# A trunk step whose late stage is queued in another order, with convolution taps issued singly and block products reordered

## The chip, the cores and the metric

The kernel runs on one core of a Trainium2 chip. The metric is the device time of one execution in microseconds (us). The engines that matter are TensorE (PE in the profile; its weight loads are PEld), VectorE (DVE), ScalarE (ACT), GpSimd (POOL) and SyncE (SP), whose queue issues most transfers. Each engine works through its own queue strictly from first to last; semaphores hold an instruction back until what it reads is written and what it overwrites has been read.

## The reference

One inference step of a two-layer trunk for 576 tokens (512 of a prompt, 64 of eight sample sequences), 1024 wide. Layer 0 is a gated short convolution, layer 1 an mLSTM with four heads of 512; each branch is 2048 wide and gated by a SiLU path z.

```python
for layer in range(DEPTH):                       # DEPTH = 2
    hnorm = rmsnorm(x, norm_w[layer])
    out = short_conv_mixer(...) if layer % 2 == 0 else mlstm_mixer(...)
    x = x + out
y = rmsnorm(x, final_norm_w)

# layer 0                                        # layer 1
b, c, xa, z = split(h @ w_in, 4)                 xm, z = split(h @ w_in, 2)
y = b * conv(c * xa) * silu(z)                   xc = silu(conv(xm) + conv_b)
out = y @ w_out                                  q, k, v = xc @ w_q, xc @ w_k, xm @ w_v
                                                 # per head: scores with decays, running state C, n, m
                                                 num = w_inter * (q @ C) + S @ v
                                                 C_new = decay * C + kw.T @ v
                                                 out = (layernorm(num / den) * onorm + skip * xc) * silu(z)
                                                 out = out @ w_out
```

The states C (4 heads x 8 samples of 512 x 512) are read, updated and written.

## The kernel before

Activations lie transposed: a tile is 128 channels by 576 tokens. Every fp32 product is made of three products of rounded parts (hi·hi, hi·lo, lo·hi), which give fp32 accuracy: a tile is cast to `hi` on ACT (L159, L202, L250) and the rest `lo` or `wl` is taken on DVE (L160, L203, L251). A chunk of weights (1024 x 128) times an activation is 48 matmuls on PE (`products`, L222), 8 blocks by three parts by two token ranges.

Stages by time in the trace: projection of layer 0 until about 375 us; its output projection until about 512; xm of layer 1 until about 611; V until about 835; K and Q until about 1290; and then the **late stage**: the z tiles of layer 1 (`z_tile`), scores, numerators (`num`), the outputs per head (`head_out`), the updates of the state C streamed through the core in 512 KB halves (load `c<-cs`, product `r` L1122, update on DVE L1123, store `cs_out`), the final states of the prompt (`cp`), and the output projection in two halves (`first_half` adds the residual x1s, `second_half`).

Names that matter below:

- `block_pair` (L290 to L365) makes two chunks of a product with seven block products instead of eight (38 pairs in layer 0, V, K and Q). Each product is 12 matmuls (L304) into one of four PSUM buffers `b0` to `b3`; DVE sums tiles of weights and adds the PSUM buffers up in 128 x 288 pieces (`tt`). `plain` (L368) makes a chunk of an ordinary product beside it.
- `work` is a queue of small closures; `run(n)` pops n of them, and `products` pops one behind the blocks named in `pops`, so that small work lands between matmuls.
- `conv_steps` / `conv`: the first tap of a convolution runs on ACT, the other three on DVE (L440 on the prompt, L442 on the samples). In layer 1, `mix` does one tile's convolution.
- `stack` (L1024 cast on ACT, L1025 on DVE) makes the parts of a tile stand beside each other; `value_stack(h)` makes `vst` for the state products, `key_stack` makes `kst`, from which `pn` (L1061) and the masked keys `km` (ACT, L1069) follow.
- `head_out(h, et)` transposes sample rows (`hb`, L1243) and prompt rows (`ha`, L1252) on PE, moves them to a tile y on ACT (L1246, L1254), adds skip * xc (DVE, L1257; `ld<-xcs` is its load) and multiplies by z (L1258). `split_out(f)` then splits that y (L159, L160), as an operand of the output projection.
- The large accumulators `acc` have two PSUM buffers; a z tile's is emptied by one ACT instruction (L875, SiLU once the SiLU table is loaded, before that a copy), the ones of the output projection by a DVE add (L1284).

The program is not issued as written. A scheduler lists the instructions of each engine in an order that it finds with a model of its own; what is written sets priorities and the allocation of buffers. The order of the changed program can therefore differ at places that the diff doesn't name, and stay where the diff moves code.

Of the kernel before, what the change touches and what calls it, by code (L numbers as in the profile page):

```python
# [21 lines left out]
NH = 4  # L22
# [45 lines left out]
def trunk(tc, io):  # L68
    nc = tc.nc
    ctx = ExitStack()  # L70
    with ctx:
# [103 lines left out]
        def run(n=1):  # L175
            for _ in range(min(n, len(work))):
                work.popleft()()

        stream = deque()
        clock = [0.0, None]  # L180

# [108 lines left out]
        def block_pair(c1, c2, fs, xs, out1, out2, add, mid=None, then=None, pops=0):  # L290

            a11, a12, a21, a22, s1, s2 = ahead_of.pop((c1, c2))
            o11, o12, o21, o22 = out1[:, 0:HT], out1[:, HT:NT], out2[:, 0:HT], out2[:, HT:NT]
            pu = X(name="pu")
            p, u = pu[:, 0:HT], pu[:, HT:NT]
            tt = nc.vector.tensor_tensor

            def product(bank_, w, form, start):  # L300
                for j in range(4):
                    hi, lo = fs[j][form]
                    for i, (a, x) in enumerate(((w[0], hi), (w[0], lo), (w[1], hi))):
                        nc.tensor.matmul(bank_, a[:, j, :], x, start=(start and j == 0 and i == 0), stop=(j == 3 and i == 2),  # L304
                                         skip_group_check=True)

            b1 = block("p6")
            product(b1, parts_of(s2), "t2", True)
            b0 = block("p1")
            product(b0, parts_of(a11), "b11", True)  # L310
            nc.scalar.copy(p, b0)
            run(pops)
            b2 = block("p5")
            product(b2, parts_of(s1), "t1", True)
            if add:
                tt(o12, o12, b1, ALU.subtract)
                tt(o12, o12, p, ALU.add)
            else:
                tt(o12, p, b1, ALU.subtract)
            run(pops)  # L320
            product(b0, parts_of(a12), "b21", False)
            if add:
                tt(o22, o22, b2, ALU.subtract)
                tt(o22, o22, p, ALU.subtract)
            else:
                tt(o22, p, b2, ALU.add)
            tt(a21, a21, a11, ALU.add)
            tt(s2, s2, a12, ALU.add)
            run(pops)
            product(b1, parts_of(a21), "t3", False)  # L330
            run(pops)
            b3 = block("p4")
            product(b3, parts_of(a22), "t4", True)
            tt(u, b1, p, ALU.subtract)
            if add:
                tt(o22, o22, b1, ALU.add)
            else:
                tt(o22, b1, o22, ALU.subtract)
            run(pops)
            product(b2, parts_of(s2), "b22", False)  # L340
            if mid:
                mid()
            if then:
                block_weights(*then)
            if add:
                tt(o11, o11, b0, ALU.add)
                tt(o21, o21, b3, ALU.add)
                tt(o21, o21, u, ALU.add)
            elif xs is None:
                nc.scalar.copy(o11, b0)  # L350
                tt(o21, b3, u, ALU.add)
            else:
                plain(b3, b1, c2 + 1, xs, False)
                tt(o21, b3, u, ALU.add)
                tt(o22, b1, o22, ALU.add)
                plain(b0, b2, c1 + 1, xs, None)
                nc.scalar.copy(o11, b0)
            tt(o12, o12, b2, ALU.add)

        def plain(ba, bb, chunk, xs, start):  # L360

            w = weights(chunk)
            for k in range(8):
                (hi, lo), (xh, xl) = w[k // 4], xs[k]
                for i, (a, x) in enumerate(((hi, xh), (hi, xl), (lo, xh))):  # L365
                    for b, t in ((ba, 0), (bb, HT)):
                        new = start if t == 0 or start is None else True
                        nc.tensor.matmul(b, a[:, k % 4, :], x[:, t:t + HT], start=bool(new) and k == 0 and i == 0,  # L368
                                         stop=(k == 7 and i == 2), skip_group_check=True)
                if k % 2:  # L370
                    run()

        def gemm_pair(c1, c2, fs, xs, out1, out2, plain_first=False, mid=None, then=None):

# [242 lines left out]
        for f in range(NW):  # L617
# [14 lines left out]
            elif f % 2:  # L632
                fm.append(forms(us[f - 1], u))

            def mix(f=f, u=u, ext=ext, ext_f=ext_f):
                cv = T(name="xc")
                conv(cv, u, ext_f, [col(f"cb{j}", f) for j in range(4)])
                nc.gpsimd.tensor_copy(cpb[:, f, :], u[:, NP - 3:NP])
                nc.scalar.activation(cv, cv, AF.Silu, bias=col("cbias", f))
                store_act(out=xcs[f], in_=cv)  # L640
                if f % 4 == 3:
                    store(out=io["exb_out"][f // 4], in_=ext)
                if f == NW - 1:
                    store(out=io["cpb_out"], in_=cpb)

            work.append(mix)
            if f >= LAG:
                run()
            if f == NW - 3:
                block_weights(96, 98)  # L650

# [54 lines left out]
        for h in range(NH):  # L706
            vt = []
            for dt in (0, 2):
# [10 lines left out]
                if 4 <= f < 12:  # L719
                    work.extend(lambda f=8 + f - 4 + i: xc.append(split(later_tile(f))) for i in range(2))  # L720
            work.append(lambda h=h, vt=vt: gates(h, vt))

        Sc, qcs = {}, {}
        far = [dram.tile([P, 512], F32, name=f"far{i}") for i in range(3)]
# [143 lines left out]
                nc.scalar.copy(z, flat(acc))  # L868
            zs[f // 4].append(z)

        table, last_silu = [], []

        def silu(out, src):
            with tc.issue_after(table[0]):
# [2 lines left out]
        def silu_table():  # L877

            with tc.issue_after(last_exp[0].ins):
                table.append(nc.scalar.preload_act_table_set("silu_and_others").ins)  # L880
            for h in range(NH):
                for t in zs[h]:
                    silu(t, t)


        keep = T(name="keep")
# [268 lines left out]
        def preps(h):  # L1155
            work.extend(lambda jt=jt: prep_values(h, jt) for jt in range(4))
            work.extend(lambda t=t: prep_scores(h, t) for t in range(4))

        def weighted_keys(h, dt):

# [75 lines left out]
        def head_out(h, et):  # L1236

            nums = heads[h]["nums"]
            f = 4 * h + et
            if et == 0:  # L1240
                pb = bank("hb")
                for i in range(4):
# [33 lines left out]

        x2 = []

        def first_half(m):
            x = T(name="x")  # L1280
            load(out=x, in_=x1s[m])
            acc = mm("acc")
            products(acc, weights(208 + 2 * m), y2[0:8], True, True)
            nc.vector.tensor_tensor(x, flat(acc), x, ALU.add)  # L1284
            x2.append(x)

# [33 lines left out]
        for h in range(NH):  # L1320
# [49 lines left out]
            for dt in range(2):  # L1370
                fetch_keys(h + 1, dt)
            work.extend(lambda h=h, et=et: head_out(h, et) for et in range(4))
            if h == 2:
                work.extend(lambda f=f: split_out(f) for f in range(8, 12))
            z_tile((0, 1, 2, 3, 4, 5, 6, 7))
            if h == 2:
                work.append(lambda: "vst" in heads[3] or value_stack(3))
                run(len(work))
                for m in range(FH):
                    first_half(m)  # L1380


        run(len(work))
        for m in range(FH + FI, 4):
            first_half(m)
        for et in range(4):
            head_out(3, et)
        for f in range(12, 16):
            split_out(f)
        for m in range(4, KD):  # L1390
            first_half(m)

        with tc.issue_after(last_silu[0]):
            nc.scalar.preload_act_table_set("abs_reciprocal_sqrt_and_small")
# [199 lines left out]
```

## Time and profile before

| | us |
|---|---|
| median of three runs (1714.5, 1715.65, 1722.03) | 1715.65 |
| the profiled execution | 1715.56 |
| its span, first to last instruction | 1713.5 |
| PE busy | 1669.4 |
| DVE busy | 1105.3 |
| ACT busy | 685.3 |
| mean granted clock of PE, share of full speed | 0.987 |

PE is busy for 97% of the span, so the time is that of its matmuls, plus the 44 us in which it stands, plus the time in which it runs at a lower granted clock. The window tables used below give, for each stretch, its length, the busy us of each engine with the number of its instructions (x), the granted clock (1.00 is full speed), the busy share of the 16 DMA engines and GB/s.

### The profile page before, as it was taken

How to read it: one execution, taken by the hardware profiler on the slowest of the kernel's cores; microseconds unless marked ns; L12 is line 12 of the kernel's file. 1: busy time of each engine (PE TensorE's matmuls, PEld its weight loads, DVE VectorE, ACT ScalarE, POOL GpSimd, SP SyncE). 2: the span in 40 equal slices, each digit the busy share in tenths (PEclk: the TensorE clock that was granted, in tenths of full speed). 3: DMA queues.
4: the chain of work that ended last, by engine and by line, in shares of the span. 5: the costliest groups of instructions: out<-in, count | busy, mean ns of one | idle time of the engine just before them, and what ended most of it. 6: DMA issues, size and time to landing. Idle time of an engine off the chain costs nothing.

```text
span 1713.5 us, 30944 instructions
## 1 busy us (share of the span) xinstructions
PE 1669.4 (97%) x12315; PEld 1591.1 (93%) x12315; DVE 1105.3 (65%) x2078; ACT 685.3 (40%) x1252; POOL 107.7 (6%) x241
## 2 busy tenths in 40 slices
PE   9999999999999999999999999999999998898998
PEld 8999999999999999999999889899899787898898
DVE  6977877774436896555846345355468556778755
ACT  5433343342323553433534233233246455554421
POOL 0000000000000001000110010000021000000000
PEclk9999999999999999999999999999999899999999
DMA  5223322223432434434423552642745588797973
GB/s 193 74 83 99 103 86 85 90 73 137 141 115 87 141 122 151 138 111 154 152 88 120 188 178 87 219 154 62 271 161 195 201 280 286 247 361 249 362 276 105
DMA packets 107487, 275.23 MB, mean 161 GB/s; under 512 B 11056, under 2 KB 33456, under 8 KB 107344
## 3 DMA queue, kind: packets, MB, share of 16 engines
q1 hardware_dynamic: 91984, 255.95, 45.0%
q10 hardware_dynamic: 15360, 17.32, 2.9%
q8 instruction: 97, 1.59, 0.4%
q14 instruction: 46, 0.38, 0.1%
HBM read 211.13 MB, written 62.09 MB: 159 GB/s over the span
## 4 chain that ended last, share of the span: by engine, by line
PE 88%; DMA 5%; DVE 4%; ACT 2%; issue 1%; SPq 0%; POOL 0%; DVEq 0%; ACTq 0%; POOLq 0%
PE acc L222 34%; PE p L304 24%; PE p L368 16%; DMA c<-cs 2%; PE qa L759 2%; PE r L1122 2%; DMA cs_out<-c 1%; DMA wr<-wts 1%; PE g L661 1%; PE num L1175 1%; PE ta L680 1%; PE cp L1175 1%; PE num L1176 1%; PE s L778 1%; PE blk L368 1%
## 5 line engine op out<-in xcount | busy, mean ns | idle before, releaser
L222 PE MATMUL acc<-hi,wh 128*128 128x256 f32 (+1 forms) x1520 | 331.7, 299 | 11.1 <-ACT z L875 6.8
L222 PE MATMUL acc<-hi,wl 128*128 128x256 f32 (+1 forms) x1520 | 330.8, 299 | 0.0
L222 PE MATMUL acc<-lo,wh 128*128 128x256 f32 (+1 forms) x1520 | 330.2, 299 | 0.0
L202 ACT CAST wh<-wr 128x512 fp32r<-128x512 f32 x286 | 176.5, 621 | 328.6 <-PE acc L222 174.5
L304 PE MATMUL p<-hi,wh 128*128 128x288 f32 x968 | 286.7, 299 | 3.7 <-ACT wh L250 2.1
L304 PE MATMUL p<-lo,wh 128*128 128x288 f32 x968 | 284.5, 295 | 0.0
L304 PE MATMUL p<-hi,wl 128*128 128x288 f32 x968 | 279.2, 295 | 1.2 <-DVE wl L251 1.2
L222 PEld LDWEIGHTS acc<-hi,wh 128*128 128x128 f32 x1520 | 257.8, 191 | 16.0 <-ACT z L875 7.0
L203 DVE TENSOR_TENSOR wl<-wr,wh 128x512 fp32r<-128x512 f32 x286 | 195.8, 689 | 118.4 <-ACT wh L202 115.8
L222 PEld LDWEIGHTS acc<-hi,wl 128*128 128x128 f32 x1520 | 257.8, 191 | 2.2 <-issue 1.2
L222 PEld LDWEIGHTS acc<-lo,wh 128*128 128x128 f32 x1520 | 257.7, 191 | 0.7 <-issue 0.5
L250 ACT CAST wh<-wr 128x512 fp32r<-128x512 f32 x152 | 94.5, 622 | 258.4 <-PE p L368 116.7
L304 PEld LDWEIGHTS p<-hi,wh 128*128 128x128 f32 x968 | 181.9, 188 | 7.8 <-ACT wh L250 3.7
L304 PEld LDWEIGHTS p<-lo,wh 128*128 128x128 f32 x968 | 182.4, 188 | 0.0
L304 PEld LDWEIGHTS p<-hi,wl 128*128 128x128 f32 x968 | 179.9, 188 | 1.4 <-DVE wl L251 1.4
L368 PE MATMUL p<-hi,wh 128*128 128x288 f32 x736 | 169.9, 299 | 0.0
L368 PE MATMUL p<-lo,wh 128*128 128x288 f32 x736 | 166.9, 294 | 0.0
L368 PE MATMUL p<-hi,wl 128*128 128x288 f32 x736 | 166.4, 296 | 0.2 <-DVE wl L203 0.2
L251 DVE TENSOR_TENSOR wl<-ws,wh 128x512 fp32r<-128x512 f32 x114 | 78.7, 691 | 119.6 <-ACT wh L250 119.4
L250 ACT CAST wh<-ws 128x512 fp32r<-128x512 f32 x114 | 70.8, 621 | 187.8 <-PE p L368 108.3
L251 DVE TENSOR_TENSOR wl<-wr,wh 128x512 fp32r<-128x512 f32 x152 | 104.9, 691 | 52.3 <-ACT wh L250 50.5
L368 PEld LDWEIGHTS p<-hi,wh 128*128 128x128 f32 x736 | 120.8, 188 | 14.7 <-issue 11.2
(371 smaller groups left out, 2557.2 us busy)
## 6 DMA issues: line engine op xcount, KB each, us to landing
wr<-wts SPq DMA_DIRECT2D x222, 512.0 KB, 3.6
c<-cs SPq DMA_DIRECT2D x112, 512.0 KB, 5.8
cs_out<-c SPq DMA_DIRECT2D x64, 512.0 KB, 6.7
x<-xT SPq DMA_DIRECT2D x16, 288.0 KB, 4.1
xcs<-xc ACTq DMA_DIRECT2D x16, 288.0 KB, 2.2
x<-xcs SPq DMA_DIRECT2D x16, 288.0 KB, 4.1
x<-x1s SPq DMA_DIRECT2D x16, 288.0 KB, 4.5
ld<-xcs SPq DMA_DIRECT2D x16, 288.0 KB, 7.5
```

The lines of the kernel that those rows point to most:

```text
L202: last_act[0] = nc.scalar.copy(hi, raw[:, 4 * i:4 * i + 4, :]).ins
L203: nc.vector.tensor_tensor(lo, raw[:, 4 * i:4 * i + 4, :], hi.bitcast(F32), ALU.subtract)
L222: nc.tensor.matmul(acc[:, o:o + j - i], a[:, k % 4, :], x[:, i:j], start=(first and k == 0 and p == 0), stop=(last and k == 7 and p == 2))
L250: last_act[0] = nc.scalar.copy(hi, src).ins
L251: nc.vector.tensor_tensor(lo, src, hi.bitcast(F32), ALU.subtract)
L304: nc.tensor.matmul(bank_, a[:, j, :], x, start=(start and j == 0 and i == 0), stop=(j == 3 and i == 2), skip_group_check=True)
L368: nc.tensor.matmul(b, a[:, k % 4, :], x[:, t:t + HT], start=bool(new) and k == 0 and i == 0, stop=(k == 7 and i == 2), skip_group_check=True)
L661: nc.tensor.matmul(g[32 * j:32 * j + 32, 0:b - a], w[:, 32 * j:32 * j + 32], tiles[j][:, a:b], start=True, stop=True)
L680: nc.tensor.transpose(pa[:, 128 * it:128 * it + 128], t[:, 128 * it:128 * it + 128], ident)
L759: nc.tensor.matmul(st["q"][32 * g:32 * g + 32, :], st["qp"][dt // 2][:, dt % 2, 128 * u + 32 * g:128 * u + 32 * g + 32], ct[g // 2][:, g % ...
L1122: nc.tensor.matmul(r, kst[2 * i + j][:, 128 * dt:128 * dt + 128], vst[:, 0:512], start=True, stop=True)
L1175: nc.tensor.matmul(acc[:, 256:512], w, b[:, 0:256], **ends)
```

## The change

Six edits: (A) `block_pair` forms its products in the order t2, b11, t1, t3, b21, t4, b22 and shares one sum `u`, which leaves out one 128 x 288 operation on DVE for each pair. (B) The loads of x1s for `first_half` are issued one chunk ahead. (C) The SiLU of the seven z tiles that were made before the SiLU table is loaded is written in `head_out`. (D) `value_stack(h)` is queued in `preps(h)`. (E) Of heads 2 and 3, `head_out` and `split_out` are queued differently around the last z tiles and the `first_half` calls. (F) The convolution taps of layer 1 are queued singly in `slow` and taken by `drip()`, five per tile while xm is made, and one per two blocks in `plain`.

```diff
+        slow = deque()
+        def drip():
+            if slow:
+                slow.popleft()()
...
+            tt(a21, a21, a11, ALU.add)
+            product(b1, parts_of(a21), "t3", False)
             run(pops)
+            tt(u, b1, p, ALU.subtract)
             product(b0, parts_of(a12), "b21", False)
+            tt(s2, s2, a12, ALU.add)
             if add:
                 tt(o22, o22, b2, ALU.subtract)
-                tt(o22, o22, p, ALU.subtract)
+                tt(o22, o22, u, ALU.add)
             else:
-                tt(o22, p, b2, ALU.add)
-            tt(a21, a21, a11, ALU.add)
-            tt(s2, s2, a12, ALU.add)
-            run(pops)
-            product(b1, parts_of(a21), "t3", False)
+                tt(o22, u, b2, ALU.subtract)
             run(pops)
             b3 = block("p4")
             product(b3, parts_of(a22), "t4", True)
-            tt(u, b1, p, ALU.subtract)
-            if add:
-                tt(o22, o22, b1, ALU.add)
-            else:
-                tt(o22, b1, o22, ALU.subtract)
             run(pops)
             product(b2, parts_of(s2), "b22", False)
...
                 if k % 2:
                     run()
+                    drip()
...
-            def mix(f=f, u=u, ext=ext, ext_f=ext_f):
-                cv = T(name="xc")
-                conv(cv, u, ext_f, [col(f"cb{j}", f) for j in range(4)])
+            def begin(f=f, u=u, ext_f=ext_f, cv=cv):
+                cv.append(T(name="xc"))
+                cv.extend(conv_steps(cv[0], u, ext_f, [col(f"cb{j}", f) for j in range(4)]))
+                cv[1]()
...
-            work.append(mix)
+            slow.extend([begin] + [lambda s=s, cv=cv: cv[s]() for s in (2, 3, 4)] + [end])
             if f >= LAG:
-                run()
+                for _ in range(5):
+                    drip()
...
-            for h in range(NH):
-                for t in zs[h]:
-                    silu(t, t)
+            raw_z.extend(t for h in range(NH) for t in zs[h])
...
+            work.append(lambda: "vst" in heads[h] or value_stack(h))
...
+            if zs[h][et] in raw_z:
+                silu(zs[h][et], zs[h][et])
...
-        def first_half(m):
-            x = T(name="x")
-            load(out=x, in_=x1s[m])
+        def first_half(m, pops=()):
+            if m + 1 < KD:
+                fetch_x(m + 1)
+            x, = fetched.pop(("x1", m))
             acc = mm("acc")
-            products(acc, weights(208 + 2 * m), y2[0:8], True, True)
+            products(acc, weights(208 + 2 * m), y2[0:8], True, True, pops)
...
-            if h == 2:
-                work.extend(lambda f=f: split_out(f) for f in range(8, 12))
             z_tile((0, 1, 2, 3, 4, 5, 6, 7))
             if h == 2:
                 work.append(lambda: "vst" in heads[3] or value_stack(3))
-                run(len(work))
+                work.extend(lambda f=f: split_out(f) for f in range(8, 12))
+                fetch_x(0)
                 for m in range(FH):
-                    first_half(m)
+                    first_half(m, (0, 2, 4, 6))
...
-        for et in range(4):
-            head_out(3, et)
-        for f in range(12, 16):
-            split_out(f)
+        work.extend(lambda et=et: head_out(3, et) for et in range(4))
+        work.extend(lambda f=f: split_out(f) for f in range(12, 16))
         for m in range(4, KD):
-            first_half(m)
+            first_half(m, (0, 3, 6))
+        run(len(work))
```

How the instructions stand on an engine before and after is shown at three places. Numbers in names tell buffers apart and differ between the two programs; line numbers of the changed kernel are 2 to 14 higher.

ACT's queue around the last z tile, before (about 1543 to 1556 us in the trace). `z_17838<-acc` empties the last z tile's accumulator; `hi<-y` are the casts of `split_out(8)` to `split_out(11)`:

```order
L1246 ACTIVATE y_17737<-hb_17726,cols 128x64
L1254 ACTIVATE y_17731<-ha_17739,cols 128x512
L1254 ACTIVATE y_17733<-ha_17753,cols 128x512
L1254 ACTIVATE y_17735<-ha_17767,cols 128x512
L202 CAST wh_18128<-wr_18126 128x512
L159 CAST hi_17804<-y_17731 128x576
L1254 ACTIVATE y_17737<-ha_17781,cols 128x512
L159 CAST hi_17814<-y_17733 128x576
L202 CAST wh_18132<-wr_18126 128x512
L159 CAST hi_17824<-y_17735 128x576
L159 CAST hi_17834<-y_17737 128x576
L875 ACTIVATE z_17838<-acc_17709 128x576
```

The same place after (`z_17794<-acc` is the last z tile):

```order
L1256 ACTIVATE y_17715<-hb_17704,cols 128x64
L884 ACTIVATE z_17794<-acc_17677 128x576
L1406 ACT_TABLE_LOAD
L1264 ACTIVATE y_17709<-ha_17717,cols 128x512
L1031 CAST sth_17818<-ld_17386 128x512
L1264 ACTIVATE y_17711<-ha_17731,cols 128x512
L1264 ACTIVATE y_17713<-ha_17745,cols 128x512
```

The emptying of the last z tile has moved from behind all four casts of y to in front of the moves of the `ha` transposes; the four `hi<-y` casts stand 13 to 17 rows behind it.

PE's queue in the output projection of the first halves, before (1626 to 1633 us): the last matmul of one `first_half`, the row `pn`, ten state products `r` in a row (six of them shown), and the first matmul of the next `first_half`:

```order
L222 MATMUL acc_18675<-hi_17699,wl_18683 128x320
L1061 MATMUL pn_18789<-seln,kst_18784 128x4 x4
L1122 MATMUL r_18807<-vst_17840,km_18329 128x512
L1122 MATMUL r_18811<-vst_17840,km_18330 128x512
L1122 MATMUL r_18846<-vst_17840,km_18331 128x512
...
L1122 MATMUL r_18960<-vst_17845,km_18800 128x512
L1122 MATMUL r_18995<-vst_17845,km_18797 128x512
L1122 MATMUL r_18999<-vst_17845,km_18798 128x512
L222 MATMUL acc_18755<-hi_17205,wh_18758 128x256
```

The same place after, with the last matmuls before the row and the first behind it:

```order
L228 MATMUL acc_18711<-hi_17642,wl_18719 128x320
L1068 MATMUL pn_18749<-seln,kst_18744 128x4 x4
L1129 MATMUL r_18767<-vst_17595,km_18293 128x512
L1129 MATMUL r_18771<-vst_17595,km_18294 128x512
L228 MATMUL acc_18711<-hi_17667,wh_18718 128x256
...
L228 MATMUL acc_18711<-hi_17694,wl_18719 128x320
L1129 MATMUL r_18810<-vst_17595,km_18295 128x512
L228 MATMUL acc_18818<-hi_17167,wh_18821 128x256
```

The `r` now come in ones and twos with 5 to 30 matmuls of an accumulator between them.

DVE's queue in the first pair of V, before (621 to 627 us): convolution taps (L440, L442) of four tiles between sums of the block products (L334, L338) and the low part of a weight (L203):

```order
L440 SCALAR_TENSOR_TENSOR xc_7199<-xm_6661,cols,xc_7199 128x511
L442 SCALAR_TENSOR_TENSOR xc_7199<-ext_6368,cols,xc_7199 128x64
L334 TENSOR_TENSOR pu_7021<-p_7022,pu_7021 128x288
L338 TENSOR_TENSOR v_7020<-p_7022,v_7020 128x288
L440 SCALAR_TENSOR_TENSOR xc_7224<-xm_6740,cols,xc_7224 128x511
L442 SCALAR_TENSOR_TENSOR xc_7224<-ext_6679,cols,xc_7224 128x64
L440 SCALAR_TENSOR_TENSOR xc_7248<-xm_6817,cols,xc_7248 128x511
L442 SCALAR_TENSOR_TENSOR xc_7248<-ext_6679,cols,xc_7248 128x64
L440 SCALAR_TENSOR_TENSOR xc_7175<-xm_6584,cols,xc_7175 128x510
L442 SCALAR_TENSOR_TENSOR xc_7175<-ext_6368,cols,xc_7175 128x64
L203 TENSOR_TENSOR wl_7160<-wr_7153,wh_7159 128x512
```

The same pair after:

```order
L442 SCALAR_TENSOR_TENSOR xc_7160<-xm_6570,cols,xc_7160 128x510
L444 SCALAR_TENSOR_TENSOR xc_7160<-ext_6354,cols,xc_7160 128x64
L442 SCALAR_TENSOR_TENSOR xc_7244<-xm_6647,cols,xc_7244 128x510
L209 TENSOR_TENSOR wl_7214<-wr_7207,wh_7213 128x512
L444 SCALAR_TENSOR_TENSOR xc_7244<-ext_6354,cols,xc_7244 128x64
L442 SCALAR_TENSOR_TENSOR xc_7160<-xm_6570,cols,xc_7160 128x509
L444 SCALAR_TENSOR_TENSOR xc_7160<-ext_6354,cols,xc_7160 128x64
L257 TENSOR_TENSOR wl_7288<-ws_7135,wh_7287 128x512
```

Before, the first pair of V holds the taps of six tiles; after, it holds those of two, the second pair those of two, and the third and the fourth those of one each.

## Rows read from the trace of the kernel before

**Rows 1.** The page: the busy time of each engine (busy us, share of the span, instructions).

```profile
PE 1669.4 (97%) x12315; PEld 1591.1 (93%) x12315; DVE 1105.3 (65%) x2078; ACT 685.3 (40%) x1252; POOL 107.7 (6%) x241
```

**Rows 2.** The waits of PE over the whole span, longest total first: line that waited <- line waited for, us in total, times, longest.

```profile
PE acc L222 <- ACT z L875: 6.8, 1, 6.8
PE num L1200 <- DVE vst L1025: 3.1, 1, 3.1
PE r L1122 <- ACT y L1254: 2.7, 1, 2.7
PE pn L1061 <- DVE kst L1025: 2.4, 2, 1.8
PE r L1122 <- DVE c L1123: 2.3, 10, 0.6
...
PE acc L222 <- DVE x L1284: 1.5, 1, 1.5
...
PE p L304 <- DVE wl L251: 1.2, 1, 1.2
```

**Rows 3.** Windows around the last z tile (window, length, PE, PEld, DVE, ACT and POOL busy us with instructions, granted clock, DMA share, GB/s).

```profile
1545.00:1550.00 5.00, 4.33 (x32) 4.01 (x30) 5.00 (x8) 3.75 (x7) 0.00 (x0) 1.00 0.58 226
1550.00:1555.00 5.00, 0.00 (x0) 0.00 (x0) 4.76 (x8) 0.82 (x2) 0.00 (x0) 0.84 0.43 116
1555.00:1560.00 5.00, 3.87 (x16) 3.87 (x17) 2.88 (x5) 4.19 (x8) 0.00 (x0) 0.50 0.98 336
1560.00:1565.00 5.00, 5.00 (x37) 4.87 (x36) 2.59 (x6) 3.70 (x6) 0.53 (x1) 0.98 0.09 34
```

**Rows 4.** The timeline there (start, duration, engine, line, operation, and in brackets the idle time of that engine before it and what ended it).

```profile
1554.01 0.76 DVE L1258 TENSOR_TENSOR y<-y,z 128x576 f32<-128x576 f32 x1
...
1554.86 0.67 ACT L159 CAST hi<-y 128x576 fp32r<-128x576 f32 x1 [3.32 <-DVE y L1258]
...
1555.43 0.64 ACT L875 ACTIVATE z<-acc 128x576 f32<-128x576 f32 x1
...
1556.13 0.85 PE L222 MATMUL acc<-hi,wh 128*128 128x256 f32 x2 [6.79 <-ACT z L875]
```

**Rows 5.** Windows over the end of the first halves of the output projection and behind it; columns as in rows 3.

```profile
1615.00:1620.00 5.00, 3.50 (x18) 3.19 (x19) 5.00 (x8) 0.55 (x2) 0.00 (x0) 0.83 1.04 390
1620.00:1625.00 5.00, 5.00 (x33) 4.96 (x33) 4.03 (x7) 1.20 (x2) 0.00 (x0) 0.83 0.95 349
1625.00:1630.00 5.00, 3.10 (x13) 1.83 (x12) 3.56 (x7) 3.70 (x6) 0.00 (x0) 0.85 0.99 366
1630.00:1635.00 5.00, 5.00 (x13) 3.19 (x14) 4.89 (x8) 0.00 (x0) 0.00 (x0) 0.50 1.03 410
...
1650.00:1700.00 50.00, 50.00 (x375) 49.39 (x374) 28.44 (x60) 12.82 (x27) 0.00 (x0) 1.00 0.40 130
```

**Rows 6.** The chain of work that ended last, in the same place, in order of time: start, us, what.

```profile
1580.11 8.59 DMA cs_out<-c
1588.77 6.43 DMA c<-cs
1595.20 6.32 DMA cs_out<-c
...
1602.02 7.08 DMA ld<-xcs
1609.19 0.83 DVE y L1257
...
1616.17 0.76 DVE x L1284
...
1629.10 4.00 PE r L1122 x6
...
1659.55 0.47 PE r L1122 x2
1660.02 3.99 PE acc L222 x30
```

**Rows 7.** Windows in the first pair of V; columns as in rows 3.

```profile
630.00:635.00 5.00, 4.83 (x36) 4.59 (x35) 5.00 (x12) 2.11 (x4) 0.00 (x0) 1.00 0.13 22
635.00:640.00 5.00, 3.82 (x26) 3.20 (x25) 5.00 (x13) 3.07 (x5) 0.00 (x0) 1.00 0.78 274
640.00:645.00 5.00, 3.94 (x30) 3.71 (x29) 5.00 (x11) 4.08 (x7) 2.56 (x2) 1.00 0.44 127
...
650.00:850.00 200.00, 198.65 (x1536) 194.32 (x1535) 125.42 (x232) 77.71 (x140) 13.44 (x33) 1.00 0.44 136
```

**Rows 8.** The timeline at the SiLU table load and at a set of sample numerators (`sample_numerators`, L1200); columns as in rows 4.

```profile
1411.77 4.13 ACT L875 ACTIVATE z<-z 128x576 f32<-128x576 f32 x7
...
1417.95 1.08 PE L1122 MATMUL r<-vst,km 128*128 128x512 f32 x2 [2.72 <-ACT y L1254]
...
1465.51 0.61 ACT L1024 CAST sth<-ld 128x512 fp32r<-128x512 f32 x1
...
1468.17 0.58 PE L1200 MATMUL num<-vst,pst 128*128 128x256 f32 x1 [3.13 <-DVE vst L1025]
```

**Rows 9.** A stretch of layer 0 by its window (columns as in rows 3), and the operation of DVE that the pairs share: line, engine, operation, count: shortest/median/longest ns.

```profile
100.00:400.00 300.00, 300.00 (x2260) 300.00 (x2260) 225.64 (x406) 117.45 (x199) 7.24 (x13) 1.00 0.30 92
...
L334 DVE TENSOR_TENSOR pu<-p,pu x38: 449/456/469, 63.4 to 1269.3; 128x288 f32<-128x288 f32 x38
```

More of the change, by code (lines that the diff above doesn't have):

```diff
@@ L633, in trunk, with end @@
                 fm.append(forms(us[f - 1], u))
-            def mix(f=f, u=u, ext=ext, ext_f=ext_f):
-                cv = T(name="xc")
-                conv(cv, u, ext_f, [col(f"cb{j}", f) for j in range(4)])
+            cv = []
+            def begin(f=f, u=u, ext_f=ext_f, cv=cv):
+                cv.append(T(name="xc"))
+                cv.extend(conv_steps(cv[0], u, ext_f, [col(f"cb{j}", f) for j in range(4)]))
+                cv[1]()
+            def end(f=f, u=u, ext=ext, cv=cv):
                 nc.gpsimd.tensor_copy(cpb[:, f, :], u[:, NP - 3:NP])
-                nc.scalar.activation(cv, cv, AF.Silu, bias=col("cbias", f))
-                store_act(out=xcs[f], in_=cv)
+                nc.scalar.activation(cv[0], cv[0], AF.Silu, bias=col("cbias", f))
+                store_act(out=xcs[f], in_=cv[0])
                 if f % 4 == 3:
@@ L721, in trunk @@
             work.append(lambda h=h, vt=vt: gates(h, vt))
+        assert not slow
         Sc, qcs = {}, {}
@@ L869, in z_tile @@
             zs[f // 4].append(z)
-        table, last_silu = [], []
+        table, last_silu, raw_z = [], [], []
         def silu(out, src):
@@ L1277, in trunk, with fetch_x @@
         x2 = []
-        def first_half(m):
-            x = T(name="x")
-            load(out=x, in_=x1s[m])
+        def fetch_x(m):
+            fetch(("x1", m), x1s[m], n=NT)
+        def first_half(m, pops=()):
+            if m + 1 < KD:
+                fetch_x(m + 1)
+            x, = fetched.pop(("x1", m))
             acc = mm("acc")
-            products(acc, weights(208 + 2 * m), y2[0:8], True, True)
+            products(acc, weights(208 + 2 * m), y2[0:8], True, True, pops)
             nc.vector.tensor_tensor(x, flat(acc), x, ALU.add)
```

## The prediction

> **What bounds the kernel now.** I read the page first, for the engine that sets the time: PE is busy for 1669.4 of the 1713.5 us span, DVE for 65% of it [rows 1]. The change removes no matmul, so it can win only what PE stands idle, 44 us in all, or runs below full clock: the mean granted clock of 0.987 is worth about 22 us (1.3% of 1713.5). The list of PE's waits comes next. It names where the idle time is: one wait of 6.8 us for the emptying of a z tile, one of 3.1 for `vst`, one of 2.7 for a move of y, and several of 1 to 2 us [rows 2]. Then windows and timeline of each of these places, for what made the releaser late and what the clock did behind the wait; and for the output projection the chain that ended last, since the clock there is low for 20 us with little idle time shown. In layer 0 there is nothing to win: 300.00 of 300 us busy at full clock [rows 9].
>
> **The last z tile (E).** PE stands 6.79 us until 1556.13, released by the z of L875 [rows 4]. That instruction needs only a finished accumulator, but in ACT's queue it stands behind four casts of y, and ACT itself stood 3.32 us for the last y of DVE [rows 4]. So the wait is one of queue order, not of work. Behind it PE runs at the lower level: granted 0.50 in 1555:1560, where it was busy 3.87 us [rows 3], so half of that, 1.9 us, is lost too (0.98 in the next window: then it is over). After, the z stands before the moves of `ha`, and the casts of y 13 and more rows behind it. What is late next? The casts go to the second half of the output projection alone; nothing that PE does in the next 50 us reads them. I charge 1 us for state products that follow here at the pace of DVE's update (0.6 us the longest wait of this kind [rows 2]). Gain 6.8 + 1.9 - 1 = 7.7. Bounds: 3, if half of the wait returns before another instruction, to 8.7.
>
> **The state products in the output projection (E, B).** In 1615:1635 PE is idle for 1.50 us (1615:1620) and 1.90 us (1625:1630), and the clock of the four windows is 0.83, 0.83, 0.85 and 0.50 [rows 5]: 0.85 + 0.85 + 0.75 + 2.5 = 4.95 us of full speed are missing. Together 8.4 us. Two causes lie one behind the other. The first wait, of 1.5 us for the add x of L1284 [rows 2], ends a chain of transfers: `cs_out` 8.59, `c<-cs` 6.43, `cs_out` 6.32 and `ld<-xcs` 7.08 us, and only then the y that waits for `ld`, with the add queued behind it on DVE [rows 6]. The second is the wait of `pn` for `kst`, 1.8 us [rows 2], with ten `r` in a row behind it, the last six of which take 4.00 us [rows 6], 0.67 each where two r take 0.47 elsewhere [rows 6]: they need PSUM buffers that DVE empties one by one. After, `pn` stands between matmuls of an accumulator, and the r come in ones and twos. That is the pattern of 1659.55, two r before thirty matmuls [rows 6], in a stretch with 50.00 of 50 us busy at clock 1.00 [rows 5]. So the second cause should go: 1.9 + 0.75 + 2.5 = 5.15. The first remains, since the load `ld<-xcs` keeps its place in SP's queue behind the stores of C, and the add its place behind the y on DVE. Loading x1s a chunk ahead (B) moves one 288 KB load forward in a queue that is full; x itself was not what the add waited for, so B alone is worth nothing, and costs nothing as long as the weights arrive. I take 4 of the 5.15. Bounds 0 to 8.4.
>
> **The convolution taps (F).** In the first pair of V DVE is full (5.00 of 5 in three windows) and PE misses 0.17 + 1.18 + 1.06 = 2.4 us [rows 7]; it waits there for `wl` of L251 [rows 2], which stands behind taps. After, four of six tiles' taps leave this pair for the next three. These have room: in 650:850 DVE is busy for 125.42 of 200 us [rows 7]. Gain 2.2, bounds 0 to 2.4.
>
> **Value stacks and SiLU (C, D).** The seven SiLUs stand together in both orders, 4.13 us, and PE waits 2.72 us for the y behind them [rows 8]. After, two value stacks' casts of 0.61 us each [rows 8] are queued between them and the y, and their release is mostly on ACT: I charge 0.5 us, bounds 0 to 1.5. In return the numerators that waited 3.13 us for `vst` [rows 8] find it made; but they now stand ahead of `pn` and wait for `pst`, whose cast on ACT is queued behind four masks. Part of the stall moves only: gain 1, bounds 0 to 3.1.
>
> **Block products (A).** One operation of 0.456 us [rows 9] less in each of 38 pairs is 17 us of DVE, but DVE is 225.64 of 300 us busy in layer 0 and PE never waits for it [rows 9]: worth nothing, hidden by PE. In exchange b22 must now wait until o22 has read its PSUM buffer. The order puts 37 matmuls ahead of it in layer 0 and about 28 in V, K and Q: at 0.133 us (300 us for 2260 [rows 9]) 4.9 and 3.7 us, against 0.9 us for u and o22. The cover is 4.0 and 2.8 us of other DVE work. Cost 0; if it fails, see the rivals.
>
> **Sum.** 7.7 + 4 + 2.2 + 1 - 0.5 = 14.4 us. PE then reaches the chain of transfers up to 9 us sooner, while the DMA engines are 0.95 to 1.04 busy from 1615 to 1635 [rows 5] and behind 1650 at 0.40, so these can't all follow: I give 2 us back. 12.4 off the profiled execution's 1715.56 is 1703.2; the median of the runs, 1715.65, is the same within 0.1. Forecast **1703 us**.
>
> **Rivals.**
>
> *The transfers bind.* The chain from 1580 to 1609 is 28.4 us of transfers in 29 [rows 6]. If they come no sooner, y, the add x and PE behind them stand where they stood: the gains at z and at the numerators become a longer wait at the add, and a longer pause costs another 1.9 us of clock, as in rows 3. Left are 2.2 and 4, less 0.5 and 1.9: 1715.56 - 3.8 = 1711.8. For it: DMA at 1.0 there. Against it: 0.43 and 0.09 in 1550:1555 and 1560:1565 [rows 3], slack that an earlier PE can use. Chance 0.2.
>
> *All of it comes.* With transfers ahead and the first cause in the output projection gone as well, 8.7 + 8.4 + 2.4 + 1 - 0.5 = 20: 1695.6. Against it: the place of `ld<-xcs`. Chance 0.14.
>
> *Slower: b22 waits.* Where DVE runs behind by more than the cover, each pair pays the rest. From 0.55 us a pair on (38 x 0.55 = 21 us against the 12.4 gained) the kernel is slower by over 0.5%; with both operations exposed, 38 x 0.92 = 35, it takes 1738 us. For it: DVE is 75% busy in layer 0 [rows 9] and was full from 630 to 645 [rows 7]. Against it: PE waits for DVE nowhere in 100:400, where b22 stood directly behind t3. Chance 0.07.
>
> *The clock doesn't hold between r pairs.* Every pair of r puts a short hold-up between groups of matmuls. If the granted clock stayed at 0.83, as in 1615:1625 [rows 5], over the 50 us with pairs, 8.5 us are lost: 1711.7. Against it: pairs at clock 1.00 after 1650 [rows 5, 6]. Chance 0.03. The Trainium skill (TensorE: Matmul & The Clock Gate, A second HAM failure mode: psum-queue depth-cycling) tells of a kernel that cycles through PSUM buffers and idles briefly between groups of matmuls, so that its clock swings between the two levels. By that rule this rival would be the forecast; the trace, at 1.00 with the same pattern, does not agree.
>
> *The late order gives nothing.* Other instructions take the places in front of z and r, 1715. Chance 0.06.
>
> **How the numbers follow.** The forecast has 0.5, and spans 1698 to 1708. With the rivals on the faster side the range goes from 1693 (all of it, and the whole 3.1 at the numerators) to 1715; left out are b22's case and half of the last. About 0.5% (8.6 us) is what a measurement here tells from no change. Faster than 1707: 0.9 of the forecast's 0.5 and the 0.14, with 0.03 of the transfers' rival, 0.62. Slower than 1724: b22's 0.07 and 0.02 of the last rival, should its place be a worse one, 0.09. Same: 0.29.
>
> **What would show it.** In the profile after: no wait of acc for z above 1 us and PE busy for 50 us at clock 1.00 around the last z tile (right for E); no run of ten r, and clock 1.00 where `pn` stands, with a wait for the add x left (half right) or gone; 630 to 645 full (F); no wait of L310 for DVE sums of 0.3 us or more in layer 0 and V (A). Wrong would be: a new wait over 5 us for `c`, `ld` or `y` between 1540 and 1640 with DMA at 1.0, or many waits of p for DVE in the pairs.

## The result

The changed kernel takes 1705.92 us (median; 1705.22 to 1710.66) where the kernel before takes 1720.8 in the runs beside it (1715.65 in the runs that stood ahead of the prediction). The ratio is 0.9934, with a 95% interval of 0.9917 to 0.9951 (it is taken over all runs and isn't the quotient of these two medians, 0.9914); timed a second time, beside later experiments, 0.9950 (0.9934 to 0.9966). That is some 9 to 11 us less; 12.4 was forecast. The sum is nearly right, but several of its terms are not: one of 7.7 us was worth nothing, one that was set at 0 costs 5. The experiments show which.

The profiled execution took 1710.66 us, the longest of five, and so shows some 5 us less gain than the medians. Its page, first part, answers to [rows 1]:

```profile
PE 1670.7 (98%) x12315; PEld 1592.4 (93%) x12315; DVE 1094.3 (64%) x2040; ACT 682.3 (40%) x1252; POOL 102.3 (6%) x241
```

The list of PE's waits after, longest total first, answers to [rows 2]:

```profile
PE r L1129 <- DVE c L1130: 3.7, 12, 1.5
PE acc L228 <- ACT num L1196: 3.6, 1, 3.6
PE qa L768 <- DMA c<-cs: 2.5, 3, 1.4
PE cp L1183 <- DVE lo L1174: 2.5, 2, 2.0
PE num L1183 <- DVE ld L1298: 2.2, 1, 2.2
PE ha L1262 <- ACT y L1264: 2.1, 2, 1.8
```

The three longest waits of before (6.8 for z, 3.1 for `vst`, 2.7 for y) are gone. In their place stand new ones of 2 to 4 us: for `num` on ACT, for the add of a residual on DVE (L1298), for y in front of `ha`. Where they stand is seen in windows of 50 us over the late stage, first before, then after (columns as in rows 3; the windows start at the same times, not at the same work, but the late stage begins within 1 us of the same time in both):

```profile
1400.00:1450.00 50.00, 43.84 (x299) 37.83 (x298) 35.02 (x69) 29.95 (x68) 1.19 (x5) 0.97 0.83 289
1450.00:1500.00 50.00, 44.80 (x311) 41.62 (x310) 34.59 (x69) 25.94 (x57) 3.91 (x7) 0.97 0.78 267
1500.00:1550.00 50.00, 48.73 (x361) 47.00 (x359) 39.10 (x79) 30.72 (x63) 1.57 (x3) 1.00 0.96 351
1550.00:1600.00 50.00, 43.39 (x302) 41.20 (x303) 40.17 (x85) 23.67 (x48) 2.65 (x7) 0.93 0.79 269
1600.00:1650.00 50.00, 46.39 (x293) 42.31 (x293) 31.38 (x47) 16.25 (x29) 0.00 (x0) 0.90 0.97 363
```

```profile
1400.00:1450.00 50.00, 43.65 (x281) 37.31 (x281) 36.97 (x71) 31.41 (x72) 1.12 (x5) 0.93 0.81 292
1450.00:1500.00 50.00, 48.44 (x360) 46.20 (x359) 35.11 (x74) 26.64 (x60) 2.75 (x7) 1.00 0.90 302
1500.00:1550.00 50.00, 49.02 (x353) 46.27 (x352) 32.80 (x66) 29.14 (x61) 1.56 (x3) 1.00 0.96 341
1550.00:1600.00 50.00, 40.99 (x250) 36.50 (x248) 39.24 (x81) 21.69 (x46) 2.33 (x7) 0.90 0.80 257
1600.00:1650.00 50.00, 49.84 (x365) 48.66 (x366) 37.02 (x60) 18.81 (x35) 0.00 (x0) 1.00 1.00 360
```

A window's loss is read as the idle time of PE plus its busy time times what the granted clock lacks of 1. Around the former z wait, 1550:1600, the loss is 6.6 + 3.0 = 9.6 before and 9.0 + 4.1 = 13.1 after: it grew. In 1600:1650, the state products in the output projection, it is 3.6 + 4.6 = 8.2 before and 0.2 after. In 1450:1500 it fell from 6.5 to 1.6, and in 1400:1450 it rose from 7.5 to 9.4. Over all five windows it falls from 33.2 to 25.2 us.

The z tile itself does what the changed order says: it is emptied at 1546.18, before at 1555.43 [rows 4]. The timeline after, behind it, shows what is late next (columns as in rows 4):

```profile
1546.18 0.67 ACT L884 ACTIVATE z<-acc 128x576 f32<-128x576 f32 x1
...
1550.11 0.76 DVE L1298 TENSOR_TENSOR ld<-acc,ld 128x576 f32<-128x576 f32 x1 [3.91 <-PE r L1129]
...
1561.11 0.38 PE L1183 MATMUL num<-vh,hi 128*128 128x256 f32 x1 [2.17 <-DVE ld L1298]
...
1566.96 1.07 ACT L1196 COPY num<-num 128x514 f32<-128x514 f32 x2
```

The residual's add (`ld<-acc,ld`) is at the head of DVE's queue from 1546.2 on, and DVE stands 3.91 us. The row puts that down to a matmul `r`, which the add doesn't read; its accumulator's last matmul stands in PE's queue in front of another `r`, of 1546.36. The load of x1s was issued at 1543.45; the two of the stretch 1543:1546 took 6.7 us to land, which for the first is about 1550.1, when the add starts (columns: tensor, queue, operation, count, KB each, median us to landing):

```profile
ld<-x1s SPq DMA_DIRECT2D x2, 288.0 KB, 6.7
```

In the second trace of the changed kernel, and in that of the kernel with edits B to E alone, the add's row names the load:

```profile
1546.46 0.76 DVE L1298 TENSOR_TENSOR ld<-acc,ld 128x576 f32<-128x576 f32 x1 [3.10 <-DMA ld<-x1s]
1547.18 0.76 DVE L1289 TENSOR_TENSOR ld<-acc,ld 128x576 f32<-128x576 f32 x1 [3.92 <-DMA ld<-x1s]
```

All of DVE's work behind it, the y of head 2 and the updates of C among it, has to wait as long. The chain of work that ended last goes on with ACT, which stands for a load of `kss`, with the emptying of `num` queued behind it (start, us, what):

```profile
1570.16 7.09 DMA ld<-kss
...
1577.91 0.58 ACT num L1196
```

### The profile page after: what moved, and what is told of

Same layout as the page of the kernel before. It is cut to its first block, busy times and chain, and to the rows that moved or that the text cites. A ratio compares the mean times of both kernels' runs of the same rounds, so it can differ in the third digit from the quotient of the medians.

```text
span 1708.8 us, 30842 instructions
## 1 busy us (share of the span) xinstructions
PE 1670.7 (98%) x12315; PEld 1592.4 (93%) x12315; DVE 1094.3 (64%) x2040; ACT 682.3 (40%) x1252; POOL 102.3 (6%) x241
## 4 chain that ended last, share of the span: by engine, by line
PE 89%; DMA 5%; DVE 3%; ACT 1%; issue 1%; POOL 1%; SPq 0%; DVEq 0%; ACTq 0%
PE acc L228 35%; PE p L310 24%; PE p L369 16%; DMA c<-cs 2%; PE qa L768 2%; DMA cs_out<-c 2%; PE cp L1183 1%; PE r L1129 1%; PE cp L1184 1%; PE g L669 1%; PE ta L688 1%; PE blk L369 1%; PE s L787 1%; DMA wr<-wts 1%; PE s L788 0%
```

## Experiments

Each ratio is to the kernel before, timed beside it, with its 95% interval. Two kernels whose intervals overlap much are not told apart by the time alone; then the traces are compared. A trace is one execution: the two of the changed kernel lose 25.2 and 24.4 us in 1400:1650, and their spans are 1708.8 and 1703.4 us, so a few us between single traces prove little by themselves.

**The parts alone.** The kernel before with edit F (taps) only:

```diff
...
-            work.append(mix)
+            slow.extend([begin] + [lambda s=s, cv=cv: cv[s]() for s in (2, 3, 4)] + [end])
```

> The kernel before with edit F alone (taps queued singly). My step says 2.2 us less (ratio 0.9987), all of it between 610 and 650 us: PE misses less than 0.5 us in 630:645 instead of 2.4, and the late stage is that of before, with its wait of about 6.8 us for the last z tile. A rival by which the stall only moves to the next pairs of V gives 0 and PE idle of 2 us more in 650:850.

Measured: 0.9969 (0.9956 to 0.9983), 5.3 us less. The three windows of [rows 7] are full:

```profile
630.00:635.00 5.00, 5.00 (x40) 5.00 (x39) 2.67 (x5) 1.79 (x3) 0.00 (x0) 1.00 0.34 125
635.00:640.00 5.00, 5.00 (x40) 5.00 (x40) 2.10 (x4) 2.46 (x5) 1.33 (x4) 1.00 0.34 102
640.00:645.00 5.00, 5.00 (x43) 5.00 (x42) 4.99 (x11) 3.66 (x6) 0.00 (x0) 1.00 0.65 193
...
1600.00:1650.00 50.00, 47.42 (x332) 45.47 (x331) 32.29 (x50) 16.86 (x30) 0.00 (x0) 0.97 0.98 360
```

The step holds where it was made: 2.4 us. Where the rest comes from isn't shown. The scheduler, with other work ahead, listed three state products behind `pn` instead of ten, and the loss in 1600:1650 fell from 8.2 to 4.0, though this edit doesn't touch the late stage; but 1400:1450 and 1550:1600 lose 4.4 us more, and over 1400:1650 the loss is 33.9 after 33.2.

Edit A (order of the block products) only:

```diff
+            product(b1, parts_of(a21), "t3", False)
             run(pops)
+            tt(u, b1, p, ALU.subtract)
             product(b0, parts_of(a12), "b21", False)
```

> The kernel before with edit A alone (order of block products). My step says 0 (0.999 to 1.001), DVE busy 17 us less, layer 0 still 300.00 of 300 us busy. The rival that b22 waits for the PSUM buffer that DVE reads gives waits of p for DVE in the pairs and 17 to 35 us more (1.01 to 1.02). A third view, that a lighter DVE also helps K and Q, gives up to 2 us less, since PE misses only that much between 850 and 1300.

Measured: 1.0030 (1.0017 to 1.0042), 5.1 us more. It costs, and not by the rival's mechanism: layer 0 is still full and p waits for DVE nowhere new. The last plain matmul of K and Q starts 2.2 us later; the rows give the shortest, median and longest ns, then the first and last start, before and with edit A:

```profile
L368 PE MATMUL p<-hi,wl x736: 288/294/401, 623.4 to 1284.0; 128*128 128x288 f32 x184
```

```profile
L363 PE MATMUL p<-hi,wl x736: 290/295/401, 622.5 to 1286.2; 128*128 128x288 f32 x184
```

From the starts of all matmuls between the first product of V and the last of K and Q (5055 intervals in each kernel) the stretch is 672.05 us before and 673.62 with edit A. The small gate products g stand among the block products in 14 groups before and in 16 with A. All steps from, to and among the g sum to 16.95 us before and 18.11 with A. Of the 1.16 more, 0.53 is one wait that the profile shows, for k on ACT, first before, then with A:

```profile
PE p L304 <- ACT k L382: 0.7, 1, 0.7
```

```profile
PE p L304 <- ACT k L377: 1.2, 1, 1.2
```

Another 0.27 would have been two steps between block products at 0.133. That leaves 0.36 us for two groups more. The `qa` products stand in 24 groups in both kernels; those groups and the step behind each take the same time, 23.9 us.

The larger part lies in the late stage. In 1400:1650 the loss is 33.2 us before and 37.3 with A, and with all other edits in it is 19.2 without A (the trace of the experiment "Without edit A") and 25.2 and 24.4 with it. Some 30 rows of DVE's queue and some ten of ACT's changed places there, and the ten state products in a row stay; which of the moves costs the time was not found.

Edits B, C, D and E (late stage) only:

> The kernel before with edits B, C, D and E alone (late stage). My step says 10.2 us less (7.7 + 4 + 1 - 0.5 - 2), a ratio of 0.994; the trace of the changed kernel says that the wait for the last z tile (6.8 us) and the low clock in 1610:1640 go, and that new waits of some 8 us come behind the last z tile. If the gain of the changed kernel came from the first half, this kernel gives 0 to 4.

Measured: 0.9934 (0.9917 to 0.9951), 11.4 us less; 1600:1650 is full at clock 1.00, and in 1550:1600 the loss is 6.7 + 6.1 = 12.7. The three parts multiply to 0.9969 x 1.0030 x 0.9934 = 0.9933, the ratio of the changed kernel as measured first (0.9950 the second time).

**Without edit A.** The changed kernel with the block products of before:

> The changed kernel without edit A (block products as before), all other edits in. If the parts add up as their single runs say (0.9969 for the taps, 0.9934 for the late stage), the ratio is 0.990 and edit A costs about 5 us in the changed kernel too. If A costs only in the company of the old late order, the ratio is 0.993 as in the changed kernel. My prediction had A at nothing.

Measured: 0.9911 (0.9893 to 0.9928), 1700.25 us. Against the mean of the two measurements of the changed kernel, 0.9942, A costs 5.3 us here too: its cost doesn't hang on the old late order. The two windows in which the kernels with and without A differ most are 1400:1450 (9.4 and 6.9 us of loss) and 1550:1600 (13.1 and 8.7), far behind the block products; without A:

```profile
1400.00:1450.00 50.00, 44.40 (x298) 37.92 (x299) 36.86 (x71) 30.84 (x71) 0.95 (x5) 0.97 0.79 291
1550.00:1600.00 50.00, 44.42 (x291) 40.19 (x291) 37.10 (x81) 19.35 (x42) 2.33 (x7) 0.93 0.90 294
```

**The wait for z.** The changed kernel with `split_out(8)` to `split_out(11)` queued before the last z tile again, and without the pops in the first calls of `first_half`:

```diff
+            if h == 2:
+                work.extend(lambda f=f: split_out(f) for f in range(8, 12))
             z_tile((0, 1, 2, 3, 4, 5, 6, 7))
...
-                work.extend(lambda f=f: split_out(f) for f in range(8, 12))
+                run(len(work))
                 fetch_x(0)
                 for m in range(FH):
-                    first_half(m, (0, 2, 4, 6))
+                    first_half(m)
```

> The changed kernel with the first part of E undone: split_out(8) to split_out(11) are queued before the last z tile again, so in ACT's queue the emptying of that tile stands behind three of the four casts of y; the state products stay spread out. My step on the z tile gives 7.7 us more than the changed kernel, with a wait of acc for z of 5 us or more. If the stall only changes its place (the trace of the changed kernel has 9 us of PE idle in 1550:1600 against 6.6 before), the kernel is 0 to 2 us slower.

Measured: 0.9917 (0.9899 to 0.9934), no slower than the changed kernel; against the mean of that one's two measurements it is 4 us faster, with intervals that overlap. Yet the wait is back, as long as ever; first of its waits of PE between 1400 and 1640, then two windows:

```profile
PE acc L228 <- ACT z L884: 7.0, 1, 7.0
```

```profile
1500.00:1550.00 50.00, 45.59 (x325) 42.51 (x323) 35.85 (x69) 28.58 (x60) 1.56 (x3) 1.00 0.91 320
1550.00:1600.00 50.00, 45.39 (x319) 42.95 (x320) 39.31 (x84) 24.20 (x48) 2.73 (x7) 0.93 0.87 299
```

The loss of both windows is 4.4 + 4.6 + 3.2 = 12.2 us; in the changed kernel 1.0 + 9.0 + 4.1 = 14.1. The z tile's wait was the place where PE stood for work of DVE and ACT that is late anyway. Taken away there, at least the same time is waited for the residual, `num` and the state products.

**The value stacks.** The changed kernel without edit D:

```diff
-            work.append(lambda: "vst" in heads[h] or value_stack(h))
```

> The changed kernel with edit D undone (value stacks not queued in preps). My step had D and C together at a gain of 0.5 us: a wait of 3.1 us for vst of the numerators should come back, and 0.5 us at the SiLU table load should go. If vst is what set the numerators, this is 2.5 to 4 us slower; if their stall only moved, the same within 1 us.

Measured: 0.9917 (0.9900 to 0.9935). Again the wait is back and the time is not longer (again 4 us shorter than that mean, with intervals that overlap); PE's wait, then the window in which the wait stands and the one in which the changed kernel lost 13.1 us:

```profile
PE num L1207 <- DVE vst L1032: 3.7, 1, 3.7
```

```profile
1450.00:1500.00 50.00, 44.63 (x305) 41.39 (x304) 35.63 (x71) 26.18 (x58) 2.63 (x7) 0.93 0.81 285
1550.00:1600.00 50.00, 46.63 (x332) 42.97 (x331) 42.08 (x89) 23.05 (x48) 3.15 (x7) 1.00 0.88 307
```

The second loses 3.4 here; the first loses 8.5, after 1.6 in the changed kernel. The loss changed its place.

**Head 3's outputs, popped.** The kernel before with the second part of E only:

```diff
...
-        for et in range(4):
-            head_out(3, et)
-        for f in range(12, 16):
-            split_out(f)
+        work.extend(lambda et=et: head_out(3, et) for et in range(4))
+        work.extend(lambda f=f: split_out(f) for f in range(12, 16))
         for m in range(4, KD):
-            first_half(m)
+            first_half(m, (0, 3, 6))
+        run(len(work))
```

> The kernel before with the second part of edit E alone: head_out(3) and split_out(12..15) queued and popped in first_half(4) to first_half(7). In PE's order the run of ten state products becomes three, then ones and twos; the last z tile keeps its place behind the casts of y. My step on the state products gives 4 us less (at most 8.4); the kernels without the wait for z or for vst say that those are worth nothing net, and then this part alone holds the late stage's whole gain: 8 to 11 us less, a ratio of 0.994 to 0.995, with clock 1.00 from 1610 to 1650.

Measured: 0.9956 (0.9938 to 0.9973), 7.5 us less. The waits for z, `vst` and y stand untouched, and the output projection runs through:

```profile
PE acc L222 <- ACT z L875: 6.8, 1, 6.8
PE num L1200 <- DVE vst L1025: 3.1, 1, 3.1
PE r L1122 <- ACT y L1254: 2.7, 1, 2.7
...
PE acc L222 <- DVE x L1284: 0.7, 1, 0.7
```

```profile
1600.00:1650.00 50.00, 49.28 (x358) 47.96 (x357) 36.58 (x57) 19.38 (x35) 0.00 (x0) 1.00 1.00 373
```

The loss of this window goes from 8.2 to 0.7 us, as much as was measured; the other four windows of 1400:1650 lose 3.7 us more in this trace, whose late stage starts 3 us sooner. Of the first cause half went too, not the second alone: the wait for the add x is 0.7 us after 1.5. DMA is as busy as before, at 1.00.

The changed kernel with this part alone undone:

> The changed kernel with the second part of E undone (head 3's outputs before first_half(4) again, all else in). By the order, the state products come in threes, ones and twos all the same. If the popping is what gains, 4 to 8 us slower than the changed kernel; if the spreading of the state products is, whatever brings it about, within 1 us of it.

Measured: 0.9950 (0.9934 to 0.9967), the same as the changed kernel beside it. By PE's order the state products are spread here too. The two kernels with ten of them in a row, the one before and the one with edit A alone, lose 8.2 and 7.2 us in 1600:1650; all others, with at most four in a row, lose 0 to 1.0, and the one with the taps alone 4.0. The row of the kernel with A alone:

```profile
1600.00:1650.00 50.00, 44.11 (x284) 39.28 (x283) 35.42 (x57) 19.41 (x37) 0.00 (x0) 0.97 1.00 369
```

So the gain goes with the spreading, and several edits of this change each bring it about.

**The load ahead.** The changed kernel without edit B:

```diff
-            if m + 1 < KD:
-                fetch_x(m + 1)
-            x, = fetched.pop(("x1", m))
+            x = T(name="x")
+            load(out=x, in_=x1s[m])
```

> The changed kernel without edit B: each first_half loads its own residual tile again. I had edit B at nothing. In the trace of the changed kernel the first add of the output projection stands at the head of DVE's queue for 3.9 us, until the load of x1s lands. If the load ahead causes that, because it is queued among stores of C, this kernel is 2 to 5 us faster than the changed one; if the load is late in any case, it is the same or up to 4 us slower, with DVE idle before the same add.

Measured: 0.9955 (0.9941 to 0.9970), against 0.9934 and 0.9950: not faster, and by the ratios some 2 us slower, within the intervals. DVE waits for x1s here too, 6.1 us in three waits, the longest 4.9. So the load is late in any case, and edit B is not its cause. Then, without A, the first load issued before the last z tile:

```diff
+            if h == 2:
+                fetch_x(0)
             z_tile((0, 1, 2, 3, 4, 5, 6, 7))
...
-                fetch_x(0)
```

> As the run before, with the first load of x1s issued before the last z tile of head 2 instead of behind it. If the add of the first half stands at the head of DVE's queue for 3.9 us because that load lands late among stores of C, the wait goes and this is 2 to 4 us faster than the run before (ratio 0.988). If the DMA engines are what is short, the wait only moves to another load and the time is the same.

Measured: 0.9896 (0.9879 to 0.9912), 1697.46 us, the fastest of the study, 8 us under the changed kernel and 18 under the kernel before. Against the same kernel with the later load (0.9911) it is 2.6 us, within the intervals. The trace of the kernel with the later load puts that add's wait, 2.4 us, down to the accumulator, so the load's part in the difference isn't shown.

**Are the transfers what binds?** The changed kernel without every second store of C:

```diff
+                if n % 2:
+                    continue
                 ins = store(out=io["cs_out"]...
```

> The changed kernel without every second store of the updated state C (16 MB instead of 32 MB written to cs_out; the odd halves are left out), all else in. If the transfers of C pace the late stage, so that a stall taken away at one place comes back at another, PE's idle time and low clock between 1500 and 1600 (14 us in the trace of the changed kernel) fall to less than half, and the time by 7 us or more. If ACT's and DVE's queue order sets these stalls, it falls by less than 3 us.

Measured: 0.9947 (0.9930 to 0.9964), the same as the changed kernel beside it (0.9950). The wait of SP's queue for stores, first the changed kernel, then this one, between 1400 and 1650:

```profile
SPq L171 <- DMA cs_out<-c: 94.2, 36, 7.1
```

```profile
SPq L171 <- DMA cs_out<-c: 47.8, 18, 7.1
```

It is halved, and the loss in 1500:1600 is 13.9 us after 14.1:

```profile
1500.00:1550.00 50.00, 47.13 (x336) 45.34 (x335) 33.62 (x67) 29.08 (x60) 1.56 (x3) 0.97 0.83 275
1550.00:1600.00 50.00, 43.44 (x280) 39.20 (x280) 40.95 (x87) 22.83 (x47) 2.33 (x7) 0.93 0.72 237
```

So the amount of data isn't what the waits are traded for. That doesn't clear the transfers. SP's queue now waits for DVE's updates of C instead:

```profile
SPq L1101 <- DVE c L1132: 31.0, 10, 10.4
SPq L171 <- DVE c L1132: 21.0, 16, 6.8
```

And the load of `kss` that ACT stands for, issued in that queue, took 6.97 us to land here, too, after 7.09. In the second trace of the changed kernel it took 4.41 us, and PE's wait for `num` is 2.3 us instead of 3.6; first this kernel, then that trace:

```profile
1567.34 6.97 DMA ld<-kss
```

```profile
1567.48 4.41 DMA ld<-kss
```

What remains is the order of the queues, SP's with ACT's and DVE's, and how long single loads take to land; which of it binds was not isolated.

The changed kernel again, beside the last three:

> The changed kernel once more, beside the other runs of this call: 0.9934 of the kernel before if what was measured first holds, 0.992 if the kernels without parts of it (0.9917) are no faster than it is.

Measured: 0.9950 (0.9934 to 0.9966), 1705.99 us. The expectation set 0.992 for the case that the two kernels with one edit undone (0.9917 each) are no faster than the changed one. It came out higher: by this measurement they are 5.7 us faster, with intervals that only touch, by the first (0.9934) 2.9 us. So those two edits gain nothing and may cost some 4 us each in the company of the others; that they do isn't shown.

## Why the prediction came out right, and where it was wrong

- **The last z tile, 7.7 us: the step failed.** The mechanism was right as far as it went (z is emptied 9 us sooner), but the net is at most 0: with the wait put back the kernel is no slower. The sign that was to show E right, 50 us of busy PE at clock 1.00 there, did not come: 40.99 us at 0.90 in 1550:1600. The step that failed is "what is late next?": the prediction looked for readers of the casts of y, found none within 50 us, and charged 1 us. Late next were the residual's add at the head of DVE's queue and `num` on ACT, neither of which reads a cast of y, but both of which stand in queues that were already behind.
- **The state products in the output projection, 4 us: under-sized.** It is 7.5 us alone, and the window's loss goes to 0.2 in the changed kernel. The step "the first cause remains" was wrong: the add of x waited behind y's in DVE's queue, and those move too when head 3's outputs are spread out. A chain made of transfers didn't mean that the transfers were the limit. The 8.4 us that the step started from count some time twice: the missing clock was taken over whole windows, idle time in them included. Over PE's busy time it is 0.60 + 0.85 + 0.47 + 2.5 = 4.4, and with 3.4 idle 7.8.
- **The taps, 2.2 us: right,** 2.4 at their place. Edit F's other 3 us are not placed: its trace has 4.2 us less loss at the state products and 4.4 more at two other places of the late stage.
- **Value stacks and SiLU, a net 0.5 us: not seen.** With edit D undone the 3.1 us wait returns as 3.7 and the time doesn't rise: the stall only moved. C was not tried by itself.
- **Block products, 0: wrong by 5 us.** No DVE wait came, as argued, and the stretch of V, K and Q is only 1.6 us longer, 0.5 of it a wait for ACT. The step failed in that it looked at the pairs alone: 4 to 6 us are lost in the late stage, whose order A changes through the scheduler.
- **The 2 us for transfers:** not shown. Half of the stores taken out changed nothing.
- **The clock between pairs of state products:** full, as the row at 1659.55 had said: 1.00 in 1600:1650, with PE busy for 49.84 us. The Trainium skill's rule (TensorE: Matmul & The Clock Gate, A second HAM failure mode: psum-queue depth-cycling) does not show there.

The forecast of 1703 is within 3 us of 1705.9, and that is luck in its terms: +7.7 for z, which gave nothing, was made up for by 3.5 more at the state products and 3 more with the taps, and these were partly undone by the 5 of edit A.

## What to carry to other kernels

A long wait with one named releaser is worth its length only if the queues of the engines that feed the next work are not behind as well: look at what stands at the head of each queue after the wait, not only at who reads the late data. Two waits of 7 and 3 us here could be put back without a loss of time, while ten short operations in a row, paced by the engine that empties their buffers, went with 7.5. And where a scheduler orders the program, an edit in one stage is judged by its order in all of them: the block products lost most of their 5 us in a stage that the edit doesn't touch.

## What the runs showed that was not expected

Where the small gate products g are cut into more groups (at three places 14 in a row became 8 and 6, at one place 2 and 14 became 16), PE loses a little time with no wait shown: 0.36 us for two groups more, 0.18 each. It takes care to see it. The step from the last g of a group to the next block product is 0.31 to 0.36 us long, but most of that is the running time of the g themselves, four of which start within 0.02 us of each other; and one of the 14 or 16 such steps holds the wait for ACT that grows from 0.7 to 1.2 us.
